# Split GELU times gate: two DMA queues that swap roles every tile

## The chip, the cores and the metric

The kernel runs on one core of a Trainium2 chip. The metric is the device time of one execution in microseconds (us); the figure for the kernel before is the median of three runs.

A core has several engines with instruction streams of their own. Here VectorE (DVE), ScalarE (ACT) and SyncE (SP) take part; TensorE and GpSimd do nothing of weight. SyncE only issues transfers and waits. Transfers between device memory and the on-chip buffers are carried out by 16 DMA engines, which take their work from queues. SyncE and ScalarE each own one such queue: an engine that issues a transfer puts it into its own queue and goes on, and a semaphore counts up by 16 when the transfer has landed.

## The reference

The input x is 32 x 512 x 2048 in float32, 134.22 MB. Each row is split in two halves of 1024; the exact GELU of the first half is multiplied with the second. The output is 32 x 512 x 1024 in float32, 67.11 MB.

```python
def reference(x):
    half_dim = x.shape[-1] // 2
    x1, x2 = (x[..., :half_dim].copy(), x[..., half_dim:].copy())
    gelu_x1 = 0.5 * x1 * (1 + erf(x1 / np.sqrt(2)))
    return (gelu_x1 * x2).astype(np.float32)
```

## The kernel before

The 16384 rows are cut into 16 tiles of 1024 rows. In a tile each of the 128 partitions holds 8 consecutive rows, so a partition's share of a tile is one contiguous stretch of memory: 64 KB of input and 32 KB of output. A whole tile is an 8 MB load and a 4 MB store.

There are two input buffers (x0_tile, x1_tile) and two output buffers (o0_tile, o1_tile); tile i uses buffer i % 2 of each. For every tile:

1. ScalarE waits until the input has landed and the output buffer is free, and computes the GELU of the first half into the output buffer (line 87), in two instructions of 5 and 3 rows. Both conditions are counts of one semaphore, ready[k], to which the load into buffer k and the store out of buffer k both add.
2. VectorE multiplies the output buffer in place by the second half of the input (line 95), instruction by instruction behind ScalarE.
3. The engine that stores waits for the multiplies and issues the store (line 56).
4. The engine that loads waits for the same multiplies, after which the input buffer is free, and issues the load of tile i+2 into it (line 49).

So store i and load i+2 are issued at the same moment, the end of tile i's last multiply, by two engines. The work that a queue holds is done in the order in which it was issued there; the order of the instructions on each engine is the order of the Python loop.

In the kernel before the roles are fixed: SyncE issues all loads, ScalarE all stores but the last ones. Tile 0 is loaded in two halves, and tiles 0 and 15 are computed in pieces of 2, 2 and 4 rows and stored in two halves. The stores of tiles 14 and 15 are issued by SyncE, which has no loads left by then, and count on a semaphore of their own, tail_stored, that SyncE waits for at the end. A tiny load of ScalarE's into a scrap tile opens the program.

The functions `load` and `store` (lines 48 to 57) issue the transfers, and the loop over tiles below calls them.

## Time and profile before

| what | value |
|---|---|
| time, median of 3 runs | 469.43 us (469.3 to 469.44) |
| span of the profiled execution, first to last instruction | 467.8 us |
| VectorE busy in the span | 140.5 us (30%), 34 instructions |
| ScalarE busy in the span | 115.5 us (25%), 35 instructions |
| memory read / written | 134.22 MB / 67.11 MB |
| mean rate over the span | 430 GB/s |
| DMA pieces ("packets") | 5057 |

The page gives no time for the profiled execution other than its span, which is 1.6 us below the median of the unprofiled runs. In the page, "L87" is line 87 of the kernel, "SPq" and "ACTq" are the queues' issuing engines, q1 and q10 the queues' own numbers, and the digits of a busy row are tenths of each fortieth of the span. A DMA issue's time is from issue to landing, the time in the queue included. The DMA share is the mean busy share of the 16 DMA engines.

### The profile page before, as it was taken

To read this page: it belongs to the slowest core of one execution; us is meant where nothing else is said; L and a number is where in the kernel's file an instruction comes from. 1 tells how busy PE (TensorE), PEld (TensorE's weight loads), DVE (VectorE), ACT (ScalarE), POOL (GpSimd) and SP (SyncE) were. 2 spreads that over 40 slices of the span, in tenths; PEclk is the share of its full clock that TensorE was granted. 3 is DMA by queue.
4 is the path that set the end of the run, shared out by engine and by line. 5 is a ranking of instruction groups with operands and counts; after the bars stand their busy time and mean duration, and the time that the engine had idled before them with its cause. 6 is when DMAs were issued, how large, how long until landed. Compare 5 with 4: busy or idle time off the path is not lost.

```text
span 467.8 us, 154 instructions
## 1 busy us (share of the span) xinstructions
DVE 140.5 (30%) x34; ACT 115.5 (25%) x35; POOL 0.2 (0%) x4
## 2 busy tenths in 40 slices
DVE  0330515207051060511606115060150702507043
ACT  1320606041060410604105050050501506014060
POOL 0000000000000000000000000000000000000000
DMA  8999999999999999999999999999999999999988
GB/s 359 448 448 448 398 406 496 403 403 448 459 437 403 440 412 493 403 403 448 487 409 403 445 406 493 403 403 448 493 403 403 448 426 471 403 426 426 493 384 379
DMA packets 5057, 201.34 MB, mean 430 GB/s; under 512 B 568, under 2 KB 576, under 8 KB 576
## 3 DMA queue, kind: packets, MB, share of 16 engines
q1 hardware_dynamic: 2880, 142.61, 70.6%
q10 hardware_dynamic: 2176, 58.73, 29.1%
q14 instruction: 1, 0.01, 0.0%
HBM read 134.22 MB, written 67.11 MB: 430 GB/s over the span
## 4 chain that ended last, share of the span: by engine, by line
DMA 76%; DVE 14%; ACT 8%; ACTq 0%; SPq 0%; issue 0%
DMA out_dram<-o_tile 66%; DVE o_tile L95 14%; DMA x_tile<-in_x_dram 10%; ACT o_tile L87 8%; ACTq L119 0%; SPq L49 0%
## 5 line engine op out<-in xcount | busy, mean ns | idle before, releaser
L95 DVE TENSOR_TENSOR o_tile<-o_tile,x_tile 128x5120 f32<-128x5120 f32 (+3 forms) x34 | 140.5, 4171 | 319.7 <-ACT o_tile L87 319.7
L87 ACT ACTIVATE o_tile<-x_tile 128x5120 f32<-128x5120 f32 (+3 forms) x34 | 114.3, 3407 | 337.3 <-DMA out_dram<-o_tile 301.8
L87 ACT ACT_TABLE_LOAD x1 | 1.3, 1283 | 2.9 <-PEq L73 2.9
L142 POOL MEMSET const-bfloat16-1.0<- 128x1 bf16 x1 | 0.1, 102 | 0.0
L142 POOL MEMSET const-uint8-127<- 128x1 uint8 x1 | 0.1, 101 | 0.0
L142 POOL MEMSET const-float32-0.0<- 128x1 f32 x1 | 0.1, 99 | 0.2 <-issue 0.2
L142 POOL MEMSET const-float32-1.0<- 128x1 f32 x1 | 0.1, 98 | 0.0
## 6 DMA issues: line engine op xcount, KB each, us to landing
out_dram<-o_tile ACTq DMA_DIRECT2D x13, 4096.0 KB, 44.7
x_tile<-in_x_dram SPq DMA_DIRECT2D x2, 4096.0 KB, 16.7
out_dram<-o_tile ACTq DMA_DIRECT2D x2, 2048.0 KB, 34.4
out_dram<-o_tile SPq DMA_DIRECT2D x1, 4096.0 KB, 25.2
out_dram<-o_tile SPq DMA_DIRECT2D x2, 2048.0 KB, 7.8
x_tile<-in_x_dram SPq DMA_DIRECT2D x15, 44.4
scrap_tile<-in_x_dram ACTq DMA_DIRECT2D x1, 4.0 KB
```

What stands on the lines that cost most here:

```text
L87: nc.scalar.activation(out=o_bufs[k][:, rows, :], in_=x_bufs[k][:, rows, :half], func=GELU),
L95: nc.vector.tensor_mul(out=o_bufs[k][:, rows, :], in0=o_bufs[k][:, rows, :], in1=x_bufs[k][:, rows, half:],),
L142: nc = _bacc.Bacc("TRN2", target_bir_lowering=False, num_devices=1)
```

## The change

The function `load` takes the queue as an argument. In the loop each tile names a load queue and a store queue by the parity of the tile: for even i, SyncE loads tile i+2 and ScalarE stores tile i, as before; for odd i, ScalarE loads tile i+2 and SyncE stores tile i. The first three loads stay with SyncE, and tile 0's stores with ScalarE. The special cases for the last two tiles are gone: tile 14 is stored by ScalarE, tile 15 by SyncE, both still counted on tail_stored.

So from the load of tile 2 on, each queue takes a load and a store in turn. SyncE's queue holds: loads 0 (two halves) and 1, load 2, store 1, load 4, store 3, and so on to load 14, store 13, store 15 (two halves). ScalarE's queue holds: store 0 (two halves), load 3, store 2, load 5, store 4, and so on to load 15, store 14. The instructions of VectorE and the activations of ScalarE are the same, in the same order. What each transfer waits for, and the semaphore it counts on, are the same.

```diff
-    def load(i, rows, sem):
-        ins = nc.sync.dma_start(out=x_bufs[i % 2][:, rows, :], in_=x_t[i][:, rows, :])
+    def load(queue, i, rows, sem):
+        ins = queue.dma_start(out=x_bufs[i % 2][:, rows, :], in_=x_t[i][:, rows, :])
         counted(ins, sem, 16)
         return ins
...
-        load(0, slice(0, 4), first[0]),
-        load(0, slice(4, 8), first[1]),
-        load(1, slice(0, 8), ready[1]),
+        load(nc.sync, 0, slice(0, 4), first[0]),
+        load(nc.sync, 0, slice(4, 8), first[1]),
+        load(nc.sync, 1, slice(0, 8), ready[1]),
...
     for i in range(n_tiles):
         k = i % 2
+        load_queue, store_queue = (nc.sync, nc.scalar) if k == 0 else (nc.scalar, nc.sync)
...
             if pieces and hi % 4 == 0:
-                if last:
-                    store(nc.sync, i, slice(hi - 4, hi), tail_stored)
-                else:
-                    store(nc.scalar, i, slice(hi - 4, hi), ready[k])
+                store(store_queue, i, slice(hi - 4, hi), tail_stored if last else ready[k])
         if not pieces:
-            if i == n_tiles - 2:
-                store(nc.sync, i, slice(0, R), tail_stored)
-            else:
-                store(nc.scalar, i, slice(0, R), ready[k])
+            store(store_queue, i, slice(0, R), tail_stored if i == n_tiles - 2 else ready[k])
         if i + 2 < n_tiles:
-            nc.sync.wait_ge(mul_done, n[mul_done.name])
-            load(i + 2, slice(0, R), ready[k])
+            load_queue.wait_ge(mul_done, n[mul_done.name])
+            load(load_queue, i + 2, slice(0, R), ready[k])
```

## The prediction

> **What bounds the kernel now.** I read the page first, then the chain of work that ended last, then the busy time by stretches, cut at the starts of tiles, and last the DMA issues in the tail.

> The page's busy shares, its DMA queues and its DMA issues:

> ```profile
> DVE 140.5 (30%) x34; ACT 115.5 (25%) x35; POOL 0.2 (0%) x4
> ...
> DMA  8999999999999999999999999999999999999988
> ...
> q1 hardware_dynamic: 2880, 142.61, 70.6%
> q10 hardware_dynamic: 2176, 58.73, 29.1%
> ...
> out_dram<-o_tile ACTq DMA_DIRECT2D x13, 4096.0 KB, 44.7
> ...
> x_tile<-in_x_dram SPq DMA_DIRECT2D x15, 44.4
> ```

> No compute engine is busy for a third of the span; the 16 DMA engines are busy in all of it. q1 is SyncE's queue (it has the loads) and q10 ScalarE's. A load and the store issued beside it land together, 44.4 and 44.7 us later.

> The chain of waits, in order of time, from tile 2 to tile 4:

> ```profile
> 60.31 40.07 DMA out_dram<-o_tile
> ...
> 100.40 4.48 ACT o_tile L87
> ...
> 104.91 8.77 DVE o_tile L95 x2
> ...
> 113.70 44.67 DMA out_dram<-o_tile
> ```

> One tile costs 13.3 us of compute (100.40 to 113.70), then its store is issued. That store takes 44.67 us, although 4 MB alone need about 9.7 us at the rates below: it queues behind its predecessor for most of a period and then shares the engines with a load.

> Busy time by stretches (length; DVE, ACT and POOL busy; clock; DMA share; GB/s):

> ```profile
> 22.40:47.00 24.60, 4.42 (x1) 3.62 (x1) 0.00 (x0) 1.00 0.99 426
> 47.00:71.40 24.40, 8.76 (x2) 7.12 (x2) 0.00 (x0) 1.00 1.00 430
> 71.40:100.40 29.00, 8.76 (x2) 7.12 (x2) 0.00 (x0) 1.00 1.00 434
> ...
> 361.40:390.40 29.00, 8.76 (x2) 7.12 (x2) 0.00 (x0) 1.00 1.00 434
> ...
> 448.50:458.00 9.50, 6.74 (x3) 7.21 (x3) 0.00 (x0) 1.00 1.01 435
> ```

> The steady period is 29.0 us for 12.58 MB (one 8.39 MB load, one 4.19 MB store): 434 GB/s with the DMA share at 1.00. In the last stretch only one store runs, on one queue, and the rate is 435. So the bound is bytes through the DMA engines, whichever direction and however many queues are filled.

> These rows also give the rule by which two queues share the engines. A packet is one partition's contiguous piece: 64 KB in a full load, 32 KB in a full store, 16 KB in a half store (q1 holds 20 DMAs of 128 pieces plus 16 completions each, 20 x 144 = 2880, as the row says). If engines alternated by bytes, a 4.19 MB store would finish well before the 8.39 MB load it shares with. They land together, at 2 to 1 in bytes. From 47.0 to 71.4 a full load ran beside half a store, 10.49 MB in 24.4 us, and again both ended together, at 4 to 1. So the engines alternate piece by piece: one round is one piece from each queue, and eight rounds on each engine finish a pair.

> **The change, part by part.** Write T(i) for the end of tile i's multiply; store i and load i+2 are issued there, in both kernels. In both, the work in flight at T(i) is load i+1 and store i-1.

> *The queue orders.* Before: q1 holds load i+1, load i+2; q10 holds store i-1, store i. After, for even i: q10 holds load i+1 then store i, and q1 holds store i-1 then load i+2; for odd i with the names exchanged. So the pair sharing the engines in any period, load i+1 with store i-1, is what it was, each at the head of its own queue; the next pair stands behind, crosswise. With piece-by-piece rounds both queues finish their eight pieces together, and the next pair starts in the next round. The steady period stays 12.58 MB at 434 GB/s, 29.0 us. Cost: 0.

> *What covers it.* At T(i) the running pair still has 44.67 - 29.0 = 15.7 us to go, so no engine runs dry while new descriptors arrive. Issue to landing of the very first 4.19 MB load is 12.0 us, of which 9.7 are bytes: 2.3 us of latency, well inside 15.7. If the cover were gone, each tile would show those 2.3 us.

> *The moved issues.* Seven loads (3, 5, ... 15) go from SyncE to ScalarE, seven stores (1, 3, ... 13) the other way. An issue takes 0.36 us on ScalarE and 0.33 on SyncE. ScalarE waited for the same multiply before its store, so nothing on it starts later: its next activation waits 21.9 us for the DMA in each tile. SyncE waits only on multiplies, in their order. Each issue is at T(i), 15.7 us early. Cost: 0.

> *Store 14* goes from SyncE to ScalarE, a new wait there, ahead of tile 15's activations. ScalarE is done with tile 14 at 426.6 us; the multiply ends and store 14 is issued at 432.76; tile 15 starts at 448.51, when its DMAs land. The new issue ends about 433.1: 15.4 us of cover, cost 0.

> *The tail.* From 448.5 the 8.39 MB of stores 14 and 15 remain, in 19.3 us: 435 GB/s, with no gap to win. Before, all three stores stand on q1. After, store 14 is alone on q10, and 15's first half (issued about 455.0, when its multiplies end) may share its last rounds. Store 14 ends about 458.0, before which the half is in the queue, and the second half (issued 460.2) finds the first still running. The last byte stays at 467.8. Cost 0; bounds, from a piece's share of a shared round, under 0.5 us either way.

> *The one operation the trace hardly shows* is a queue that turns from one direction to the other. Load to store occurs once before, at store 14 behind load 15 on q1, with the other queue empty: issued at 432.76, landed 25.2 later at 457.96; load 15 was issued at 403.74 and landed 44.4 later at 448.14. That leaves 9.82 us for 4.19 MB, against 9.66 at 434 GB/s: 0.15 us at most, rounding included. Store to load never occurs; the change makes 13 of them (loads 3 to 15 each behind a store). Lower bound: nothing, or a gain up to the difference between 434 and 435 GB/s, 0.07 us in 29.0, 0.9 us over 13 periods. Upper bound: the whole 2.3 us of a first load, 13 x 2.3 = 30 us. I take 0, by the nearest row (0.15 at most, with nothing beside it) and because a stalled queue leaves the engine to the other: one queue alone ran at 435.

> [...]

> *Sum.* The profiled execution spans 467.8 us, the median is 469.43: 1.6 us lie around the span. 467.8 + 0 + 1.6 = 469.4.

> **Rivals.**

> *The turn costs something (slower).* At each of the 13 store-to-load turns both queues turn at once, so neither covers the other. For it: both end in the same round, so the cover is thin just there. Against: store 14's turn. At 0.15 us each, 13 x 0.15 = 1.9 us, 471.3. It decides from 0.94 / 13 = 0.07 us a turn; at the upper bound the time is 499.

> *The queues drift apart (slower).* If one queue falls rounds behind, loads meet loads and stores meet stores, and a load is stuck behind a late store. A round is 29.0 / 8 = 3.6 us; a tile starts when the later of its two DMAs lands, so each round of lag eats 3.6 of the 15.7 us. Only beyond four rounds do engines idle; one round uncovered in every second period is 7 x 3.6 = 25 us, 494. Against: alternation keeps a lag constant, a lag in one period falls on the other queue in the next, and load beside load or store beside store still runs at full rate (433 for loads alone: 4.19 MB between the first two landings, at which ScalarE starts, 12.79 and 22.47; 435 for stores).

> *A better mix (faster).* A turn could hide the end of one DMA under the start of another kind, and lift 434 to the tail's 435: 0.9 us, 468.5. Against: the DMA share is already 1.00, and packets alone take the time.

> **How the numbers follow.** 0.2% of 469.4 is 0.94 us, about what a measurement of this kernel can tell from no change. No change: 0.79, with 468.9 to 469.9 as its own range. Turn cost: 0.13, of which 0.11 lies beyond the bound. Drift: 0.04. Better mix: 0.04 beyond the bound. That is faster 0.04, same 0.81, slower 0.15. The predicted time is that of no change, 469.4. The range takes in the better mix at 468.5 and the turn at its nearest row, 471.3, and leaves out the dear turn and the drift.

> **What would show it.** After, the issue table should have seven full loads and seven full stores on ScalarE's queue, eight loads and seven stores of 4 MB on SyncE's (plus the halves), q1 19 x 144 = 2736 packets; landings of 44 to 45 us for loads and stores alike on both queues; tile starts 29.0 us apart, at the same times as before to 0.1 us; the DMA share at 1.00 in each; the last store's landing 7.6 us after its issue. A turn cost would show as periods of 29.1 us and more with a share below 1.00. Drift would show as loads and stores of one issue time landing a round (3.6 us) or more apart. I am wrong if the alternation of pieces depends on which queue holds the load, or if a turn drains an engine.

## The result, and the profile after

The changed kernel takes 483.69 us (median of 4 runs, 482.94 to 483.91) against 469.44: a ratio of 1.0303, 95% interval 1.0291 to 1.0315. It is 3% slower, 14.3 us, and outside the predicted range of 468.5 to 471.3. The profiled execution spans 482.6 us, 14.8 more than before.

The page after, in the lines that answer to those shown of before (busy time, DMA share in fortieths, the queues with pieces, MB and share, the issues with the median us to landing):

```profile
DVE 140.5 (29%) x34; ACT 115.5 (24%) x35; POOL 0.2 (0%) x4
...
DMA  8999999999999999999999999999999999999988
...
q1 hardware_dynamic: 2736, 109.05, 53.1%
q10 hardware_dynamic: 2320, 92.28, 45.7%
...
out_dram<-o_tile SPq DMA_DIRECT2D x7, 4096.0 KB, 43.4
out_dram<-o_tile ACTq DMA_DIRECT2D x7, 4096.0 KB, 46.8
...
x_tile<-in_x_dram SPq DMA_DIRECT2D x8, 44.1
x_tile<-in_x_dram ACTq DMA_DIRECT2D x7, 46.9
```

Compute is the same to 0.1 us. The queues hold what was forecast: 2736 pieces on SyncE's, seven loads and nine stores (two of them half stores) on ScalarE's. The DMA engines still count as busy throughout, but the same 201 MB now occupy them for 53.1 + 45.7 = 98.8% of 482.6, 476.8 us, where they took 99.7% of 467.8, 466.4 us. So 10.4 of the 14.8 us are pieces that take longer; a full digit row hides that, since a piece that is held up counts as busy (the load pieces from 130.2 us on for 3.5 us each in place of 2.42). And what stands on ScalarE's queue lands later: loads after 46.9 us against 44.1 on SyncE's, stores after 46.8 against 43.4.

The chain of waits after, in order of time (the steps that begin at 114.25 and 174.09 end the waits of tiles 5 and 7):

```profile
60.52 40.42 DMA x_tile<-in_x_dram
...
114.25 46.52 DMA x_tile<-in_x_dram
...
160.79 4.48 ACT o_tile L88
...
174.09 47.00 DMA x_tile<-in_x_dram
```

From tile 3 on its DMA steps are 46.5 to 48.2 us where before they were 44.7, and all of them are loads of odd tiles: those that ScalarE issues. The busy time by stretches from tile start to tile start (length; DVE, ACT, POOL busy; clock; DMA share; GB/s), tile 2's start first. A piece counts in the stretch in which it starts, so a share can pass 1.00:

```profile
71.65:100.96 29.31, 8.76 (x2) 7.12 (x3) 0.00 (x0) 1.00 1.04 447
100.96:130.21 29.25, 8.76 (x2) 7.12 (x3) 0.00 (x0) 1.00 0.96 412
130.21:160.79 30.58, 8.76 (x2) 7.12 (x2) 0.00 (x0) 1.00 1.03 429
160.79:190.14 29.35, 8.76 (x2) 7.12 (x2) 0.00 (x0) 1.00 1.03 433
190.14:221.11 30.97, 8.76 (x2) 7.13 (x3) 0.00 (x0) 1.00 0.96 411
...
463.26:482.60 19.34, 8.92 (x3) 7.21 (x3) 0.00 (x0) 1.00 0.82 344
```

Every second period is long, 30.6 and 31.0 us in place of 29.0: those in which an odd tile's load (5, 7, ...) runs on ScalarE's queue beside a store on SyncE's. The others last 29.3 us or so. The last stretch is as long as before, 19.34 us, but for another reason: its share is 0.82, and only 344 GB/s x 19.34 us = 6.65 MB start in it. Before, the share was 1.01 up to 458.0 and then

```profile
458.00:467.80 9.80, 2.18 (x1) 0.00 (x0) 0.00 (x0) 1.00 0.89 382
```

So after, some engines have less left to do there than others. The trace's records of single pieces say more (they do not name the engine; I group them by sixteens in order of start). A turn is where one load-and-store pair ends and the next begins, and each queue goes over to the other direction; q1 is SyncE's queue, q10 ScalarE's; the last column is what each of the next two pieces takes beyond its usual 2.42 us (64 KB), 1.21 (32 KB) or 0.61 (16 KB), mean of 16 engines. (In the kernel before, no queue changes direction there.) A completion is one of the 16 pieces of 4 bytes that the records have at the end of each transfer (320 for the 20 transfers on SyncE's queue before).

```
kernel, turn at us      last two pieces     next two pieces      beyond usual, us
before, 100             load q1, store q10  load q1, store q10   0.00, 0.00
after, 159.6            store q1, load q10  load q1, store q10   0.00, 0.00
after, 129.2            load q1, store q10  store q1, load q10   0.30, 1.09
after, 71.0 (first)     load q1, 16K st q10 store q1, load q10   0.01, 0.12
```

So at 129.2 us one kind of turn loses 1.4 us, and at 159.6 the other kind loses nothing. The records also show that pieces do alternate one by one (before, sixteen each of q10, q1, q10 and q1 start from 98.3, 99.5, 101.9 and 103.1 us), in these two kernels with q1 first in every round. Seven turns are of the lossy kind, ahead of loads 3, 5, ..., 15, the first a mild one. The 16 completions of one full load, which before lie 0.3 to 0.4 us apart, are 0.7 apart for load 4 and 4.4 for load 15: the engines also lose step with one another, and a tile waits for the last of them (load 15's completions come from 458.4 to 462.8 us, and tile 15 starts at 463.26).

The records give an account of the whole loss, as means of the 16 engines (idle time is where fewer than 16 pieces run). Compared with before, pieces run over by 10.6 us more (10.4 by the page's rounded shares), and an engine stands idle 4.0 us longer: 14.6 of the 14.8 us. At the seven turns lie 10.9 of them, 0.2 at the first and 1.4 to 2.1 at each of the others. Of that, 1.6 us is idle time: at the later turns one to six engines at a time have nothing running, some for over 2 us, ahead of the load's first piece, although that load was issued 13 us or more before. Another 2.4 us are idle time in the last stretch, where nine engines are through with store 14 by 468.5 us and wait until 470.6 for the first half of store 15. The rest, 1.3 us, are small overruns elsewhere.

### The profile page after: what moved, and what is told of

Same layout as the page of the kernel before. It is cut to its first block, busy times and chain, and to the rows that moved or that the text cites. A ratio compares the mean times of both kernels' runs of the same rounds, so it can differ in the third digit from the quotient of the medians.

```text
span 482.6 us, 154 instructions
## 1 busy us (share of the span) xinstructions
DVE 140.5 (29%) x34; ACT 115.5 (24%) x35; POOL 0.2 (0%) x4
## 2 busy tenths in 40 slices
DMA  8999999999999999999999999999999999999988
## 3 DMA queue, kind: packets, MB, share of 16 engines
q1 hardware_dynamic: 2736, 109.05, 53.1%
q10 hardware_dynamic: 2320, 92.28, 45.7%
## 4 chain that ended last, share of the span: by engine, by line
DMA 76%; DVE 14%; ACT 8%; ACTq 0%; SPq 0%; issue 0%
DMA x_tile<-in_x_dram 76%; DVE o_tile L96 14%; ACT o_tile L88 8%; ACTq L114 0%; SPq L49 0%
## 5 line engine op out<-in xcount | busy, mean ns | idle before, releaser
L96 DVE TENSOR_TENSOR o_tile<-o_tile,x_tile 128x5120 f32<-128x5120 f32 (+3 forms) x34 | 140.5, 4171 | 334.5 <-ACT o_tile L88 334.5
## 6 DMA issues: line engine op xcount, KB each, us to landing
out_dram<-o_tile SPq DMA_DIRECT2D x7, 4096.0 KB, 43.4
out_dram<-o_tile ACTq DMA_DIRECT2D x7, 4096.0 KB, 46.8
x_tile<-in_x_dram SPq DMA_DIRECT2D x2, 4096.0 KB, 16.6
x_tile<-in_x_dram SPq DMA_DIRECT2D x8, 44.1
x_tile<-in_x_dram ACTq DMA_DIRECT2D x7, 46.9
```

The costliest lines, as they stand in the source:

```text
L96: nc.vector.tensor_mul(out=o_bufs[k][:, rows, :], in0=o_bufs[k][:, rows, :], in1=x_bufs[k][:, rows, half:],),
```

## The experiments

Median times; each ratio is to the kernel before, measured beside the run (469.27 to 469.38 us). The edits are shown abridged, against the changed kernel, that of e4 against the kernel before; the semaphores and scrap tiles that a tiny transfer needs are left out. Letters name theories, as the expectations introduce them. Where an expectation speaks of a piece that takes a turn in a queue, it means its place in a round.

**Fixed roles, exchanged (e1).**

```diff
-load_queue, store_queue = (nc.sync, nc.scalar) if k == 0 else (nc.scalar, nc.sync)
+load_queue, store_queue = nc.scalar, nc.sync
 # the opening load on SyncE, loads 0 and 1 on ScalarE
```

> Fixed roles, exchanged: ScalarE issues every load (3 to 15 and the first ones too), SyncE every store; no queue ever changes direction. Theory A (the time is lost where one engine serves two store pieces in a row, the last of one queue and the first of the other, and the next load piece then runs late): no such place exists here, so 469.4 us, tile starts 29.0 apart. Rival B (loads are slow on ScalarE's queue): the changed kernel lost 14 us with seven full loads there, so fifteen lose 25 us or more, 490 to 500. Rival C (a queue that changes direction loses time): 469.4, as A.

469.28 us, ratio 1.000 (0.999 to 1.0009). A period of it:

```profile
100.30:129.30 29.00, 8.76 (x2) 7.12 (x2) 0.00 (x0) 1.00 1.00 434
```

Loads are not slow on ScalarE's queue: B falls.

**The changed kernel with the queues exchanged (e2).**

```diff
+load_queue, store_queue = (nc.scalar, nc.sync) if k == 0 else (nc.sync, nc.scalar)
 # the opening load on SyncE, loads 0 and 1 on ScalarE; stores of tile 15 on SyncE
```

> The changed kernel with the two queues exchanged from the first transfer on: ScalarE loads tiles 0 and 1, 2, 4, ..., SyncE 3, 5, .... Only the last tile's stores stay on SyncE. Theory A: the order in a round follows the queue that had the first load, so the two stores in a row come again ahead of loads 3, 5, ..., which are now SyncE's; 482 to 485 us in all, and the long periods are those of loads 3, 5, ..., 15 on SyncE's queue. Rival B: slow loads stay with ScalarE's queue, so the long periods become those of loads 2, 4, ..., 14. Rival C: 482 to 485, with no say on which periods.

483.73 us, ratio 1.0308 (1.0285 to 1.0331). Tile starts 3 to 7:

```profile
100.87:130.13 29.26, 8.76 (x2) 7.12 (x2) 0.00 (x0) 1.00 0.96 412
130.13:160.38 30.25, 8.76 (x2) 7.12 (x2) 0.00 (x0) 1.00 1.03 433
160.38:189.87 29.49, 8.76 (x2) 7.12 (x2) 0.00 (x0) 1.00 0.98 418
189.87:220.12 30.25, 8.76 (x2) 7.13 (x3) 0.00 (x0) 1.00 1.00 425
```

The long periods are again those of tiles 5 and 7, now loaded on SyncE's queue. At 129 us the two pieces are 0.33 and 0.98 over. The loss follows the order of the pieces, as A said, and no queue.

**One swap (e3).**

```diff
+load_queue, store_queue = (nc.sync, nc.scalar) if i < 8 else (nc.scalar, nc.sync)
```

> One swap of roles only: as before for tiles 0 to 7, exchanged from tile 8 on and left so (load 10 and later from ScalarE, store 8 and later from SyncE). Theory A: one place with two stores in a row, ahead of load 10; the seven of the changed kernel cost 14.3 us, 2.0 each, and the first of them least, so 470.5 to 471.5 us, with one long period and 29.0 in all others. Rival B: six loads on ScalarE's queue at 2 us each, about 481. Rival C (each change of direction costs): 470 to 471.5, as A.

470.66 us, ratio 1.0028 (1.0017 to 1.0038). Tile starts 7 to 11:

```profile
216.45:245.46 29.01, 8.76 (x2) 7.12 (x2) 0.00 (x0) 1.00 1.00 434
245.46:274.73 29.27, 8.76 (x2) 7.12 (x2) 0.00 (x0) 1.00 0.96 412
274.73:305.08 30.35, 8.76 (x2) 7.12 (x2) 0.00 (x0) 1.00 1.02 425
305.08:334.02 28.94, 8.76 (x2) 7.13 (x3) 0.00 (x0) 1.00 0.99 428
```

One turn is the whole loss: 0.3 us in the period that ends with it and 1.35 in the next, then 29.0 again. The five further loads on ScalarE's queue cost nothing. The two slow pieces are 0.33 and 1.06 us over, together the 1.4 us by which the run is longer. B, which had 481 here, falls again.

**A tiny load behind each load, fixed roles (e4).**

```diff
             load(i + 2, slice(0, R), ready[k])
+            nc.sync.dma_start(out=tiny[:, i * 32 : i * 32 + 32], in_=x_t[0][:16, 0, :32])
```

> The kernel before, fixed roles, with a tiny load (16 partitions x 128 B, 28 KB in all) issued by SyncE behind each of the loads 2 to 15. Nothing changes direction; the tiny load and its completion take two turns of SyncE's queue, so in each period from tile 3 on the engines serve three or four store pieces in a row before the next load. Theory A: 13 such places at 1.5 to 2.1 us or more, 489 to 497 us. Rivals B and C: the loads stay on SyncE's queue and no queue turns, so 469.4 to 470.5 us (28 KB are 0.1 us at 434 GB/s).

474.73 us, with single runs from 470.0 to 482.0; ratio 1.0056 (1.0027 to 1.0084) by the six runs below 475. The trace is of a run of 477.3. Theory A had 489 to 497 and fails as this run put it: at 100 us the engines serve four store pieces in a row, and the load piece behind them is 0.03 us over. B and C had 469.4 to 470.5, which only two of the ten runs meet, but nothing here speaks for a loss that they describe. What makes this kernel slow and unsteady was not found. Its engines go out of step (completions of one load up to 9 us apart late in the run), and of the 8 us that the traced run takes beyond before, 6.4 are engines standing idle in the last 36 us; pieces run over by only 1.4 more.

After this I held D: a load piece needs time after the store piece on its own queue.

**Everything from tile 3 on in halves (e5), and the same with fixed roles (e6).**

```diff
-            store(store_queue, i, slice(0, R), ...)
+            for r in (0, 4):
+                store(store_queue, i, slice(r, r + 4), ...)
-            load(load_queue, i + 2, slice(0, R), ready[k])
+            for rows in (slice(0, R),) if i == 0 else (slice(0, 4), slice(4, 8)):
+                load(load_queue, i + 2, rows, ready[k])
 # e6: also load_queue, store_queue = nc.sync, (nc.scalar if i < 14 else nc.sync)
```

> The changed kernel with every load from tile 3 on and every full store from tile 1 on issued as two of 4 rows, on the same queues as before the cut: pieces of 32 KB and 16 KB, the same pairs, the same turns. Theory D (a load piece behind a store piece on its own queue cannot run until about 2.5 us after that store piece; one load piece of the other queue in between, 2.42 us, hides it, one store piece, 1.21 us, hides half): the pieces in between are now 1.21 and 0.61 us, so it shows at all 13 turns, 1.2 to 1.9 us each, and the time is 487 us or more. Theory A, in what the tiny loads left of it (two store pieces in a row from different queues): half as much store time in a row as a load before met for nothing, so 469.4 to 476.

> The same cut into two of 4 rows with the roles fixed as before, which prices the smaller pieces alone: 469.4 to 470.5 under both theories, since no queue turns from store to load and none has two store pieces next to another queue's.

e5: 470.44 us, ratio 1.0026 (1.0017 to 1.0035). e6: 470.85, ratio 1.0034 (1.0021 to 1.0046), a little above the 470.5 that was expected. Tile starts 3 to 6 of e5:

```profile
100.28:129.35 29.07, 8.76 (x2) 7.12 (x2) 0.00 (x0) 1.00 0.98 424
129.35:158.45 29.10, 8.76 (x2) 7.12 (x2) 0.00 (x0) 1.00 1.02 441
158.45:187.50 29.05, 8.76 (x2) 7.12 (x2) 0.00 (x0) 1.00 0.99 424
```

With half-size pieces the swapping of roles costs nothing: all turns are there, in the same order, and no piece at the turn of 129 us is over its time. D fails, and with it C: changing direction cost nothing by itself here, as the other kind of turn in the changed kernel had shown (0.00 us over at 159.6). Halving itself costs about 0.1 us a period, in both.

**One queue for everything (e7).**

```diff
+load_queue, store_queue = nc.sync, nc.sync
```

> All loads and all stores on SyncE's queue alone: store i, load i+2, store i+1, load i+3 and so on, one after the other, with work in the queue at all times. Theory D: each of 14 loads stands directly behind a store with nothing in between, so about 2.5 us (or what is left of it) is lost at each, 13 to 14 times: 500 to 505 us. Theory A: no second queue, no stores of two queues in a row, and one queue alone ran at 433 to 435 GB/s, so 469.4 to 470.

474.85 us, ratio 1.0119 (1.0103 to 1.0134): neither 470 nor 500. Each of 14 loads stands right behind a store, and its first piece is not late (0.00 us over at 139.6). The stretches that hold most of load 1, of the two half stores, of store 1 and of load 3, one after the other:

```profile
22.40:41.70 19.30, 4.42 (x1) 3.62 (x1) 0.00 (x0) 1.00 0.95 380
41.70:51.40 9.70, 3.70 (x1) 7.12 (x2) 0.00 (x0) 1.00 0.95 405
...
71.00:80.70 9.70, 3.67 (x1) 7.12 (x2) 0.00 (x0) 1.00 1.00 432
80.70:100.00 19.30, 5.09 (x2) 0.00 (x0) 0.00 (x0) 1.00 1.01 435
```

The loss lies elsewhere: load 1's last piece, ahead of half stores, is 1.34 us over on average, and later loads' last pieces, ahead of full stores, some 0.1. Why, I can't say. In all, pieces run over by 2.8 us more than before and engines stand idle 2.5 us longer, at the end of the run. It denies D a second time.

**One tiny load, once (e8).**

```diff
+            if i == 1:
+                nc.scalar.dma_start(out=tiny[:, :], in_=x_t[0][:16, 0, :32])
             load(load_queue, i + 2, slice(0, R), ready[k])
```

> The changed kernel with one tiny load (16 partitions x 128 B), once, on ScalarE's queue ahead of load 3. It takes two turns there, so from then on ScalarE's queue runs two rounds behind SyncE's. Theory D: between ScalarE's last store piece and its next load piece there are now two store pieces of SyncE's (2.4 us), and between SyncE's a load piece, so the loss shrinks to 0.3 us a turn or less: 469.4 to 472. Theory A: around each such turn both queues now serve stores for several rounds, five or six store pieces in a row from both, so the loss is at least what it was: 483 or more.

469.87 us, ratio 1.0022 (1.0006 to 1.0038); two of the ten runs took 472.2 and 472.9. Stretches of two tiles each:

```profile
100.00:158.00 58.00, 17.52 (x4) 14.25 (x4) 0.00 (x0) 1.00 1.00 434
158.00:216.10 58.10, 17.52 (x4) 14.25 (x4) 0.00 (x0) 1.00 1.01 437
```

That is 29.0 a tile with full-size pieces and all turns of roles. One 2 KB transfer gives back 13.8 of the 14.3 us: it sets the queues two rounds apart, so that they no longer turn in the same round. At 132.8 us a load piece follows six store pieces of both queues and is 0.00 over. A had said 483 or more here. D had 469.4 to 472, which the time meets, but e5 and e7 deny D; what the two queues do in the same round is what changed.

**Apart in the other way (e9), and apart on half of the engines (e10).**

```diff
 # e9, ahead of stores 1 to 13, on the storing queue:
+store_queue.dma_start(out=tiny[:, c], in_=scrap[:, :32])
 # e10: e8 with out=tiny[:8], in_=x_t[0][:8, 0, :32]
```

> The changed kernel with a tiny copy between two on-chip tiles (16 partitions x 128 B) on the storing queue ahead of each of the stores 1 to 13. Its two turns let the other queue go two pieces ahead, so the queues turn two rounds apart: the load starts right behind the last store piece of its own queue (only a last store piece or a 0.03 us copy in between), and no more than one full store piece stands before it where SyncE turns to stores. Theory D (a load needs time after the store on its own queue): it is lost at all 13 turns, 1.5 us or more each, 490 and up. Theory E (the loss is made only where both queues turn in the same round and the two next pieces after the last store are a store, then a load): 469.4 to 471.

> The kernel with the one tiny load ahead of load 3, but the load covers 8 partitions, so that its turn falls to 8 of the 16 DMA engines only; the other 8 turn as in the changed kernel. If the loss is made inside each engine: those 8 still lose what they did, the slowest of them sets the tile, and the time is 479 or more. If it is made where the engines meet (memory, all 16 turning at once): with half of them two rounds away it shrinks, and the time is below 475.

e9: 476.96 us, ratio 1.0167 (1.0137 to 1.0196). Both theories miss the time. At the turns E is right (the first two load pieces behind the store of their own queue at 129 us are 0.00 and 0.01 over), but small overruns are spread over many load pieces, more of them as the engines go out of step: 3.7 us more than before in all, and 4.0 us of idle engines, nearly all in the last 28 us. Why they go out of step was not found.

e10: 480.89 us, ratio 1.0244 (1.0229 to 1.0260). More than the 479 of the first case, yet it isn't the first case: in the records the eight engines that are set apart lose too, 1.7 us on the load piece which in e8 was on time, and the other eight lose again, 0.9 to 1.0 us, just then. What one engine's pieces take depends on what the others do at the time, so at least part of the loss is made where the engines meet.

**A tiny copy on the single queue, ahead of each load (e11) or each store (e12).**

```diff
 # e7, and ahead of each load (e11) or of each store from 1 on (e12):
+nc.sync.dma_start(out=tiny[:, c], in_=scrap[:, :32])
```

> The kernel with everything on SyncE's queue, and between each store and the load behind it a tiny copy between two on-chip tiles (16 partitions x 128 B). Theory F (an engine starts to read a piece a small, fixed number of queue entries before its turn, and completions and tiny pieces fill entries like large ones; where only one store piece or less lies in them, the load's read starts late): with the store's completion, the copy and its completion in front, the load is read only after the store's last piece, and some 1.5 to 2.6 us are lost at each of the 14 loads: 495 to 511 us. Theory G (the loss belongs to two queues that turn against each other in the same round): one queue, no loss beyond the 474.9 that it took without the copies: 474 to 476.5.

> The same with the tiny copies between each load and the store behind it, so that the loads follow the stores directly again: the control for the copies themselves. [...] Theory G: 474 to 476.5.

474.67 and 475.00 us, ratios 1.0116 (1.0101 to 1.0131) and 1.0110 (1.0090 to 1.0129). The copies do nothing (474.85 without them). F, which had 495 to 511 us for e11, falls, and it was my best account of why a load could be read late.

**Another order of the tiles (e13).**

```diff
+    at = [(5 * i) % n_tiles for i in range(n_tiles)]
 # loads from x_t[at[i]], stores to o_t[at[i]]
```

> The changed kernel with the tiles taken in another order of the memory (step i works on tile 5 i mod 16), so that the addresses that meet at each turn of the queues are others; everything else is the same. Theory H (the loss comes from where in memory the two stores and the load of a turn lie): another loss per turn, and a time that leaves the 482 to 485 of the changed kernel by several us. Theory J (it comes from the order of the pieces alone): 482 to 485 us and the same long periods.

484.52 us, ratio 1.0311 (1.0277 to 1.0345), with long periods of 30.7 to 32.4 us again, though not all at the same tiles (5, 7 and 9, then 10, 12 and 14; tile 3's is 30.9): by the time, H falls, as far as it is about which tiles meet at a turn. The spacing of the 128 pieces within a tile is the same in this run and was not varied by itself.

**Little compute (e14, e15).**

```diff
 # e14: row lo of each step alone; the other rows set to zero at the start
 # e15: the same from tile 2 on, tiles 0 and 1 in full
-            rows = slice(lo, hi)
+            rows = slice(lo, hi if i < 2 else lo + 1)
```

> The changed kernel with the computation cut to the first row of each step (2 of 8 rows in most tiles; the other output rows are zeros or leftovers), so that a tile's work takes about 3 us in place of 13.3, its transfers are issued some 10 us earlier, and the engines hardly touch the on-chip memory when the queues turn. Theory K (the compute that starts at a turn, or the short lead of the issues, makes the loss): 467 to 470 us. Theory J (order of the pieces alone): the loss stays, 481 to 485.

> The changed kernel with tiles 0 and 1 computed in full, so that the start and the meeting of the queues stay as they were, and from tile 2 on only the first row of each step (the other output rows hold what an earlier tile left). Transfers are issued some 10 us earlier from tile 2 on, and ScalarE and VectorE touch the on-chip memory for 3 us a tile, not 13. Theory K (the compute that starts at a turn, or the short lead of the issues, makes the loss): 467 to 470 us, all tile starts 29.0 apart. Theory J (the order of the pieces alone): long and short periods as in the changed kernel, 481 to 485.

e14 took 473.73 us, ratio 1.0096 (1.0079 to 1.0113), which neither theory had, and tells nothing of the turn: its other start moved the queues apart (tiles 2 to 4 start at 76.96, 103.69 and 135.02 us, 26.7 and 31.3 apart), so that no two turn in the same round, and no lossy turn occurred. e15 kept the start: 484.16 us, ratio 1.0312 (1.0292 to 1.0332), the two pieces at 129 us over by 0.32 and 0.96. Neither most of the compute nor a longer lead of the issues changes the loss: K falls.

**Halves in odd steps alone (e16).**

```diff
+            for rows in (slice(0, 4), slice(4, 8)) if k else (slice(0, R),):
 # around the store of tile i and around the load of tile i + 2
```

> The changed kernel with the transfers of odd steps alone cut into two of 4 rows (stores 1, 3, ... on SyncE's queue and the loads issued beside them, 3, 5, ..., on ScalarE's); those of even steps stay whole. At a lossy turn ScalarE's last store piece is then 32 KB as before, SyncE's first store piece 16 KB and the load piece 32 KB. Theory M (the loss grows with the bytes stored in a row there, as the first turn hints, where 16 and 32 KB met and the period was only 0.3 us longer): 469.5 to 472. Theory N (what was stored last on the load's own queue decides, 32 KB as before): 1.4 us or more a turn again, 479 or more.

479.37 us, ratio 1.0227 (1.0206 to 1.0248). At 129 us the store piece is 0.35 over and the next load pieces 0.10 and 0.12, about 0.7 in all with the small ones behind: half of what full pieces lose. Neither M nor N at the turn, though the time is just within N's; later in the run, pieces away from the turns run over as well. With the first turn (16, then 32 KB: 0.13) it suggests that the piece stored last before the turn weighs more than the one stored first after it; but in e16 the load pieces are smaller too, and the first turn is a single case.

What the runs say of the turn, from the records at 129 us unless marked:

```
kernel              last store, next store, next load, KB   beyond usual, us
after               32, 32, 64                              1.4
e3 (274 us)         32, 32, 64                              1.4
e2, e15             32, 32, 64                              1.3
e16                 32, 16, 32                              0.7
after, first turn   16, 32, 64                              0.1
e5                  16, 16, 32                              0.0
e8 (132.8 us)       32, 32, 64, two rounds apart            0.0
```

## Why the prediction was wrong

- *What bounds the kernel* was right: bytes through the DMA engines, 434 GB/s, pieces alternating one by one. In e1, e3 and e8 every undisturbed period is 29.0 us.
- *The queue orders, the moved issues, store 14 and the tail* were right in that the pairs are the same and that each transfer is issued in good time; in e15, with issues some 10 us earlier, nothing changes. The tail takes the forecast 19.3 us, but by luck: less is left to move in it, and engines that are ahead wait in it.
- *The step that failed* is the turn of the queues, "I take 0, by the nearest row (0.15 at most, with nothing beside it) and because a stalled queue leaves the engine to the other". One of the two kinds of turn costs 1.4 us where the engines are in step (129 us, e3) and up to 2.1 later; the other kind costs nothing. The nearest row was a load-to-store turn with one queue empty, which is another operation; and the second reason is untrue here: at the turn of 129 us no engine took a further piece of q1 while q10's load piece ran 1.1 us over, and at later turns engines stood idle ahead of that piece. Its rival ("the turn costs something", because both queues turn at once) came closest to the mechanism, priced by that row at 0.15 instead of 1.4 to 2.1, with a count of 13 where 7 are lossy: those seven make 10.9 of the 14.8 us. Of the sign named for it, the longer periods came; a share below 1.00 did not, because a piece that is held up counts as busy. Its other sign, "if a turn drains an engine", came in part: engines idle at the later turns.
- *The upper bound* of that step, 2.3 us a turn and 30 us in all, held the cost of every turn; the range left it out because one row seemed to exclude it. A thing that the trace never shows, done 13 times, on a path with no slack, is no place for the lower end alone.
- *Drift* was held to be unlikely, and the queues did not drift apart. What drifted apart were the 16 engines, which no rival had: completions of one load from 0.7 to 4.4 us apart. It adds 2.4 us of idle time in the last stretch, seen in its share of 0.82. With one turn alone (e3) the completions went from 0.4 to 0.8 us apart and stayed there.

The cause inside the DMA engines stays open. Shown: the 1.4 us of a turn come where both queues turn in the same round, so that the next piece of one is a store behind the other's store (e2, e3), and go when the queues turn two rounds apart (e8) or the pieces are half as large (e5). They come from neither queue (e1, e2), nor from the order of the tiles in memory (e13), nor from most of the compute (e15), nor from a run of stores (e8), nor from a store ahead of a load on one queue (e7); and the engines influence each other in it (e10). Not shown: why engines go out of step with one another, as they also do in e4 and e9, whose traced runs are 8 us longer than before without any such turn. Not tried: stores to another place than the memory off chip.

## What to carry to other kernels

Where two queues are kept full and run in step, leave each its direction: with these pieces an exchange of roles is free where a load comes next and costs 1.4 us or more where a store comes next, and seven of the second kind cost 3%. If roles must change, try halving the pieces (e5) or setting the queues two rounds apart with one tiny transfer (e8), and look at the tile starts; a tiny transfer in every period was no cure (e9, 477.0 us). And an operation that the trace has never shown is priced by its bounds, not by the nearest row that happens to be cheap.
